# Add + gelu on one core: y in three loads instead of four, a new split of the adds, and a new order of VectorE's work around chunk 9

## Chip, cores, metric

The kernel runs on one core of a Trainium2 chip. The metric is the device time of one execution in microseconds (us). "Span" is the time inside one profiled execution; it is 1.5 to 1.9 us shorter than the metric for the same run.

Four words are used throughout. The profile counts 16 DMA engines for the core (its page gives the packets' time as a share of 16); a packet is one row of a DMA as one of them moves it. Each DMA here has 128 rows, and in the packet records they start in eight rounds of 16: eight for each DMA engine. A DMA lands when all of its data have arrived. Its lead is the time by which it is issued before the DMA ahead of it in the queue lands. A hand-over is the change from one DMA of the queue to the next.

## The reference

```python
batch, dim = 1024, 4096            # x and y are float32 [1024, 4096]
z = x + y
out = 0.5 * z * (1 + tanh(sqrt(2 / pi) * (z + 0.044715 * z**3)))    # float32
```

32 MiB are read (33.55 MB) and 16 MiB written (16.78 MB).

## The kernel before

Each of the 128 partitions holds 32768 columns of x. The sum and the result are made in place in `z`. The work goes in chunks of 2048 columns: an add (VectorE or GpSimd), `mag` = |z| and `gelu` = gelu(-|z|) on ScalarE into PSUM, and `end` = max(z, 0) + that, on VectorE. All DMAs are issued from one engine's queue, SyncE, in a fixed order.

```python
    YS = 8192                       # columns of one y buffer; two buffers
    CH = 2048
    PS = 2                          # PSUM buffers
    xloads = [16384, 16384]
    yloads = [8192, 8192, 8192, 8192]
    FIRST = 8
    stores = [16384, 10240, 6144]
    # chunk added by VectorE: the `end` in front of which it stands
    by_dve = {0: 0, 2: 0, 4: 2, 6: 4, 8: 8, 12: 10}
    # ... (cut)
    def store(i):
        a, b = sr[i]
        ins = nc.sync.dma_start(out=ov[:, a:b], in_=zt[:, a:b])
        if i == 0:
            tc.add_manual_dep(
                ins.ins, ends[FIRST].name, ...,
                reason="the stores join the queue when the last load is nearly done",
            )

    def add(c):
        eng = nc.vector if c in by_dve else nc.gpsimd
        eng.tensor_add(out=zt[:, a:b], in0=zt[:, a:b], in1=yt[s][:, o : o + b - a])
    # ... (cut)
    sp = [(load_y, 0), (load_x, 0), (load_y, 1), (load_x, 1), (load_y, 2), (load_y, 3)]
    sp += [(store, i) for i in range(len(stores))]
```

## Time and profile before

| | kernel before |
|---|---|
| time, median of 3 | 120.1 us (120.07 to 120.13) |
| span of the profiled run | 118.6 us |
| busy: VectorE, ScalarE, GpSimd | 50%, 51%, 47% |
| DMA queue busy | 98.6% |
| fourth y load lands | 79.85 us |
| stores issued at | 77.61, 96.34, 107.56 us |

Read it from the bottom. The last three rows say that the queue always has work and that every store is handed to it a few us (2.2 to 3.7) before it runs out. The engines' shares say little: they are averages over a first quarter with no compute at all and a rest with a good deal of it. The lines are in the prediction below.

### The profile page before, as it was taken

Reading aid. Unit: us, or ns where it says so; the run is one execution under the profiler, and the core shown is the slowest. Engines: PE = TensorE matmul, PEld = TensorE weight load, DVE = VectorE, ACT = ScalarE, POOL = GpSimd, SP = SyncE. Lnnn points to the kernel's source line nnn. Section 1 sums busy time; section 2 is a strip of 40 time slices with the busy share of each in tenths; the row PEclk is TensorE's granted clock in tenths of the full one; section 3 lists DMA queues with packets and bytes.
Section 4 is the critical chain, followed back from the end, with each engine's and each line's share of the span. In section 5 each row is a group of like instructions: output and inputs, shape, how many; then the busy total and the mean of one; then the engine's idle time right before and its main releaser. Section 6 shows DMA issues by size and latency. Waiting matters only on the chain.

```text
span 118.6 us, 160 instructions
## 1 busy us (share of the span) xinstructions
DVE 59.8 (50%) x24; ACT 60.8 (51%) x34; POOL 55.5 (47%) x14
## 2 busy tenths in 40 slices
DVE  0000000000399999699994594257999457742000
ACT  5000000000067979999379705797798999940000
POOL 0000000000399999997000029999999999100000
DMA  7989888998889988988899898998899889999996
GB/s 243 464 365 696 354 354 354 663 398 354 354 387 497 531 354 354 707 354 354 354 420 464 365 520 354 531 531 354 354 531 531 354 354 442 442 442 442 398 398 265
DMA packets 1296, 50.33 MB, mean 424 GB/s; under 512 B 144, under 2 KB 144, under 8 KB 144
## 3 DMA queue, kind: packets, MB, share of 16 engines
q1 hardware_dynamic: 1296, 50.33, 98.6%
HBM read 33.55 MB, written 16.78 MB: 424 GB/s over the span
## 4 chain that ended last, share of the span: by engine, by line
DMA 48%; POOL 34%; POOLq 4%; ACT 3%; DVE 2%; issue 0%; SPq 0%; DVEq 0%
POOL z L149 34%; DMA z<-in_x_dram 26%; DMA y<-in_y_dram 21%; POOLq L213 4%; DVE z L166 2%; ACT w L154 2%; ACT w L157 2%; SPq L132 0%; POOLq L149 0%; DVEq L166 0%
## 5 line engine op out<-in xcount | busy, mean ns | idle before, releaser
L149 POOL TENSOR_TENSOR z<-z,y 128x2048 f32<-128x2048 f32 x10 | 55.3, 5563 | 45.6 <-DMA z<-in_x_dram 31.1
L154 ACT ACTIVATE w<-z 128x2048 f32<-128x2048 f32 x16 | 30.1, 1880 | 42.5 <-DVE z L149 36.0
L166 DVE SCALAR_TENSOR_TENSOR z<-z,w 128x2048 f32<-128x2048 f32 (+1 forms) x17 | 36.4, 2157 | 16.0 <-ACT w L157 16.0
L149 DVE TENSOR_TENSOR z<-z,y 128x2048 f32<-128x2048 f32 x6 | 24.0, 4009 | 30.3 <-DMA z<-in_x_dram 30.1
L157 ACT ACTIVATE w<-w 128x2048 f32<-128x2048 f32 x16 | 29.8, 1862 | 0.5
L198 ACT ACT_TABLE_LOAD x1 | 1.3, 1283 | 1.3 <-PEq L230 1.3
L197 DVE MEMSET one<- 128x1 f32 x1 | 0.1, 59 | 1.3 <-PEq L230 1.3
L198 ACT ACTIVATE one<-one 128x1 f32<-128x1 f32 x1 | 0.2, 203 | 0.0
L230 POOL MEMSET const-float32-0.0<- 128x1 f32 x1 | 0.1, 98 | 0.2 <-issue 0.2
L230 POOL MEMSET const-bfloat16-1.0<- 128x1 bf16 x1 | 0.1, 101 | 0.0
L230 POOL MEMSET const-uint8-127<- 128x1 uint8 x1 | 0.1, 101 | 0.0
L230 POOL MEMSET const-float32-1.0<- 128x1 f32 x1 | 0.1, 98 | 0.0
## 6 DMA issues: line engine op xcount, KB each, us to landing
y<-in_y_dram SPq DMA_DIRECT2D x4, 4096.0 KB, 23.7
out_dram<-z SPq DMA_DIRECT2D x1, 5120.0 KB, 14.9
out_dram<-z SPq DMA_DIRECT2D x1, 3072.0 KB, 11.0
z<-in_x_dram SPq DMA_DIRECT2D x2, 44.9
out_dram<-z SPq DMA_DIRECT2D x1, 21.6
```

Source lines behind the costliest of these rows:

```text
L149: eng.tensor_add(out=zt[:, a:b], in0=zt[:, a:b], in1=yt[s][:, o : o + b - a])
L154: nc.scalar.activation(out=wt[c], in_=zt[:, a:b], func=act.Abs)
L157: nc.scalar.activation(out=wt[c], in_=wt[c], func=act.Gelu_apprx_tanh, scale=-1.0)
L166: ins = nc.vector.scalar_tensor_tensor(out=zt[:, a + o : a + o + n], in0=zt[:, a + o : a + o + n], scalar=0.0, in1=wt[c][:, o : o + n], op ...
L197: nc.vector.memset(one, 0.0)
L198: nc.scalar.activation(out=one, in_=one, func=act.Gelu_apprx_tanh)
L213: tc.compile()
L230: nc = _bacc.Bacc("TRN2", target_bir_lowering=False, num_devices=1)
```

## The change

The intent: one DMA fewer and a y buffer as large as fits, so that chunks 8 and 9 don't wait for a y load and only chunks 10 to 16 depend on the last one. Three of GpSimd's adds now wait for one of VectorE's (`turn`), so that the two engines run into each other less often: in the kernel before, while one of them added, an add of the other waited (VectorE's took 2.28 us alone and up to 6.59, GpSimd's 4.50 and up to 6.64; the prediction reads this from the trace). VectorE gets more of the last adds, and it ends chunk 9 before it adds chunks 10 and 11.

```diff
-    YS = 8192
+    YS = 20416
-    yloads = [8192, 8192, 8192, 8192]
-    FIRST = 8
+    yloads = [8192, 12224, 12352]        # the third over columns 0.. of the same buffer
+    FIRST = 9
-    ... [CH] * (TOT // CH)
+    ... [CH] * 9 + [CH - 64, 64] + [CH] * 6
-    by_dve = {0: 0, 2: 0, 4: 2, 6: 4, 8: 8, 12: 10}
+    by_dve = {0: 0, 2: 0, 4: 3, 6: 5, 10: 10, 11: 10, 12: 11, 14: 12, 16: 14}
+    turn = {1: 0, 13: 12, 15: 14}        # GpSimd's add waits for VectorE's
...
-                ends[FIRST].name,        # store 0 waits for half an `end` of chunk 8
+                gelus[FIRST].name,       # store 0 waits for half a `gelu` of chunk 9
...                                       # the halves move from `end` to `gelu`
```

Because of the chunk of 64 columns, later chunks have numbers one higher than before: 17 chunks, 0 to 16.

More of the change, by code (lines that the diff above doesn't have):

```diff
@@ L104, in ranges @@
         return [(e - f, e) for e, f in zip(ends, sizes)]
-    xr, yr, sr, cr = (ranges(r) for r in (xloads, yloads, stores, [CH] * (TOT // CH)))
+    xr, yr, sr, cr = (ranges(r) for r in (xloads, yloads, stores, [CH] * 9 + [CH - 64, 64] + [CH] * 6))
     C = len(cr)
-    by_dve = {0: 0, 2: 0, 4: 2, 6: 4, 8: 8, 12: 10}
+    by_dve = {0: 0, 2: 0, 4: 3, 6: 5, 10: 10, 11: 10, 12: 11, 14: 12, 16: 14}
+    turn = {1: 0, 13: 12, 15: 14}
     def over(rs, lo, hi):
@@ L114 @@
     pool_sb = ctx.enter_context(tc.tile_pool(name="xz", bufs=1))
-    pool_y = ctx.enter_context(tc.tile_pool(name="y", bufs=2))
     pool_w = ctx.enter_context(
@@ L120, with at_y @@
     zt = pool_sb.tile([P, TOT], fp32, tag="z", name="z")
-    yt, wt, ends = {}, {}, {}
+    yt = pool_sb.tile([P, YS], fp32, tag="y", name="y")
+    wt, adds, gelus = {}, {}, {}
+    def at_y(a):
+        return a - (yr[2][0] if a >= yr[2][0] else 0)
     def load_x(i):
@@ L128, in load_y @@
         a, b = yr[i]
-        s, o = divmod(a, YS)
-        if o == 0:
-            yt[s] = pool_y.tile([P, YS], fp32, tag="y", name=f"y{s}")
-        nc.sync.dma_start(out=yt[s][:, o : o + b - a], in_=yv[:, a:b])
+        o = at_y(a)
+        nc.sync.dma_start(out=yt[:, o : o + b - a], in_=yv[:, a:b])
     def store(i):
@@ L146, in add @@
         a, b = cr[c]
-        s, o = divmod(a, YS)
+        o = at_y(a)
         eng = nc.vector if c in by_dve else nc.gpsimd
-        eng.tensor_add(out=zt[:, a:b], in0=zt[:, a:b], in1=yt[s][:, o : o + b - a])
+        ins = eng.tensor_add(
+            out=zt[:, a:b], in0=zt[:, a:b], in1=yt[:, o : o + b - a]
+        )
+        adds[c] = ins.ins
+        if c in turn:
+            tc.add_manual_dep(
+                ins.ins,
+                adds[turn[c]].name,
+                mybir.DependencyInfo(mybir.DependencyClass.Sync, mybir.DependencyReason.DATA),
+                reason="the two engines take turns on their shared port",
+            )
     def mag(c):
         a, b = cr[c]
-        wt[c] = pool_w.tile([P, CH], fp32, tag="w", name=f"w{c}")
+        wt[c] = pool_w.tile([P, b - a], fp32, tag="w", name=f"w{c}")
         nc.scalar.activation(out=wt[c], in_=zt[:, a:b], func=act.Abs)
     def gelu(c):
-        nc.scalar.activation(
-            out=wt[c], in_=wt[c], func=act.Gelu_apprx_tanh, scale=-1.0
-        )
+        w_c = cr[c][1] - cr[c][0]
+        n = w_c // 2 if c == FIRST else w_c
+        for o in range(0, w_c, n):
+            w = wt[c][:, o : o + n]
+            ins = nc.scalar.activation(
+                out=w, in_=w, func=act.Gelu_apprx_tanh, scale=-1.0
+            )
+            gelus.setdefault(c, ins.ins)
     def end(c):
         a, b = cr[c]
-        parts = 2 if c == FIRST else 1
-        n = (b - a) // parts
-        for o in range(0, b - a, n):
-            ins = nc.vector.scalar_tensor_tensor(
-                out=zt[:, a + o : a + o + n], in0=zt[:, a + o : a + o + n], scalar=0.0,
-                in1=wt[c][:, o : o + n], op0=alu.max, op1=alu.add,
-            )
-            ends.setdefault(c, ins.ins)
-    sp = [(load_y, 0), (load_x, 0), (load_y, 1), (load_x, 1), (load_y, 2), (load_y, 3)]
+        nc.vector.scalar_tensor_tensor(
+            out=zt[:, a:b], in0=zt[:, a:b], scalar=0.0, in1=wt[c],
+            op0=alu.max, op1=alu.add,
+        )
+    sp = [(load_y, 0), (load_x, 0), (load_y, 1), (load_x, 1), (load_y, 2)]
     sp += [(store, i) for i in range(len(stores))]
@@ L183 @@
         load_y: lambda i: [
-            (add, c) for c in over(cr, yr[i][0] - 2 * YS, yr[i][1] - 2 * YS)
+            (add, c) for c in over(cr, 0, yr[2][1] - yr[2][0]) if i == 2
         ],
         add: lambda c: [(load_x, i) for i in over(xr, *cr[c])]
-        + [(load_y, i) for i in over(yr, *cr[c])],
+        + [(load_y, i) for i in over(yr, *cr[c])]
+        + ([(add, turn[c])] if c in turn else []),
         mag: lambda c: [(add, c)] + ([(end, c - PS)] if c >= PS else []),
@@ L190 @@
         end: lambda c: [(gelu, c)],
-        store: lambda i: [(end, c) for c in over(cr, *sr[i])] + [(end, FIRST)],
+        store: lambda i: [(end, c) for c in over(cr, *sr[i])] + [(gelu, FIRST)],
     }
```

## The prediction

Its sum: 116.3 + 2.3 = 118.6 us of span before, less 0.06 for the packets, so 118.5, and 120.05 of metric.

> **What bounds the kernel now.** I read the page's busy shares and its DMA queue first. Of each line below, "x" counts instructions, and the last figure of a DMA issue is the median time from issue to landing in us.
>
> ```profile
> span 118.6 us, 160 instructions
> ...
> DVE 59.8 (50%) x24; ACT 60.8 (51%) x34; POOL 55.5 (47%) x14
> ...
> DMA  7989888998889988988899898998899889999996
> ...
> q1 hardware_dynamic: 1296, 50.33, 98.6%
> ...
> y<-in_y_dram SPq DMA_DIRECT2D x4, 4096.0 KB, 23.7
> out_dram<-z SPq DMA_DIRECT2D x1, 5120.0 KB, 14.9
> out_dram<-z SPq DMA_DIRECT2D x1, 3072.0 KB, 11.0
> z<-in_x_dram SPq DMA_DIRECT2D x2, 44.9
> out_dram<-z SPq DMA_DIRECT2D x1, 21.6
> ```
>
> No compute engine works more than half the span; the one DMA queue is busy for 98.6% of it. So the suspect is the queue: 32 MiB read and 16 MiB written. Second, the chain of waits, for landings (start, duration):
>
> ```profile
> 0.43 30.92 DMA z<-in_x_dram
> ...
> 44.68 25.46 DMA y<-in_y_dram
> ```
>
> The first x load lands at 0.43 + 30.92 = 31.35, when 4.19 + 8.39 = 12.58 MB are in. The third y load lands at 70.14, at 29.36 MB. Between them 16.78 MB took 38.79 us: 432.6 GB/s. Third, the timeline for the stores' issues:
>
> ```profile
> 77.61 30.28 SPq L136 DMA_DIRECT2D out_dram<-z  x3
> ```
>
> The third store ends its issue at 77.61 + 30.28 = 107.89, so begins it (0.33 us) at 107.56 and lands 11.0 later, at 118.56. From 31.35 to there, 37.75 MB in 87.21 us: 432.9 GB/s, with no time lost at any hand-over. Hence the sum of the whole span: 50.33 MB / 432.8 GB/s = 116.3 us, and 2.3 us of start and last receipt, together 118.6. The chain blames POOL for 34% only because it goes through waits that end before the queue runs dry. Compute matters in one way: each DMA must be issued before its predecessor is through. The second y-buffer turn and the stores are the ones that wait for compute.
>
> How early is early enough? The fourth y load lands at 79.85 (issue 57.94 from the timeline, 21.9 in the DMA view of that window); store 0 is issued at 77.61, 2.24 before that, and lands at 77.61 + 21.6 = 99.2; 79.85 + 8.39 MB / 432.8 = 99.24. So a lead of 2.24 us over the predecessor's landing leaves no gap. Store 1, issued at 96.34, has 2.9 us; store 2 has 111.24 - 107.56 = 3.7 us.
>
> Fourth, the durations of adds, and how the two adders meet:
>
> ```profile
> L149 POOL TENSOR_TENSOR z<-z,y x10: 4502/5562/6635, 31.5 to 96.8; 128x2048 f32<-128x2048 f32 x10
> L149 DVE TENSOR_TENSOR z<-z,y x6: 2280/3636/6593, 31.5 to 83.0; 128x2048 f32<-128x2048 f32 x6
> ```
>
> ```profile
> 31.45 8.80 DVE L149 TENSOR_TENSOR z<-z,y 128x2048 f32<-128x2048 f32 x2 [30.06 <-DMA z<-in_x_dram]
> 31.49 13.16 POOL L149 TENSOR_TENSOR z<-z,y 128x2048 f32<-128x2048 f32 x2 [31.06 <-DMA z<-in_x_dram]
> 33.78 1.88 ACT L154 ACTIVATE w<-z 128x2048 f32<-128x2048 f32 x1 [31.02 <-DVE z L149]
> 35.69 1.86 ACT L157 ACTIVATE w<-w 128x2048 f32<-128x2048 f32 x1
> ...
> 40.18 2.27 DVE L166 SCALAR_TENSOR_TENSOR z<-z,w 128x2048 f32<-128x2048 f32 x1
> ```
>
> An add is 2.28 us on VectorE and 4.50 on GpSimd when alone. Two VectorE adds took 8.80 = 2.28 + 4.4 + 2.2: one ran, GpSimd ran, then the other.
>
> [...] the VectorE add, when waiting, was served before GpSimd's next one. The final op (one SBUF input, one PSUM) is 2.27-2.29 throughout and does not take part. [...] this trace has only 24, 32, 40 and 64 KB rows.
>
> **The change, part by part.**
> *Traffic.* The same bytes. y goes in three loads, not four: 128 packets (8 per DMA engine) and one completion fewer. The packet records show 1.212 us for 32 KB and 2.418 us for 64 KB, so about 6 ns a packet is fixed: 8 x 6 = 48 ns, and one 9 ns completion: 0.06 us saved, on the path.
> *Landings*, if the queue never idles, at 432.8 GB/s: x0 31.35; y1 (6.26 MB) 45.8; x1 65.2; y2 (6.32 MB) 79.8; store 0 99.2, store 1 111.3, store 2 118.5.
> *y2's issue.* It overwrites columns 0 to 12351 of y, so it waits for the adds of chunks 0 to 6 (64 columns of chunk 6). Adds 0, 1, 2, 3 run as before to 44.7. Add 5 (GpSimd) waits for y1 and runs 45.9 to 50.4. VectorE ends chunk 2 at 48.7 and its add 4 is held to 50.4, runs to 52.7; end 3 to 55.0. Chunk 4's two activations take 3.75: 56.5; its end 58.8; add 6 then runs to 61.1 [...]. y2 is issued at about 61.1: lead 4.1 us over x1's 65.2, against over 15 before (44.68 against 60.4), still above 2.24.
> *Store 0.* It now needs the first half of chunk 9's gelu. x1 65.2; add 8 to 69.8; add 9 (1984 columns) to 74.2; abs 1.83 to 76.0; half a gelu 0.95: issue at 77.0. Lead 2.8.
> *After y2.* End 9 runs to 80.2, so putting it ahead of adds 10 and 11 delays them by only 0.4 past the landing. Add 10 (64 columns) 0.1, add 11 to 82.6, end 10, add 12 to 84.9, add 13 (GpSimd, told to wait for add 12) to 89.4, add 14 to 91.7, add 15 (told to wait) to 96.2. ScalarE: chunk 11 from 82.65 to 86.4, chunk 12 to 90.1, chunk 13 to 93.9. End 13 to 96.2, store 1 issued at about 96.3: lead 2.9. Add 16 to 98.5, end 14 to 100.7, chunk 16's activations 101.4 to 105.15, end 107.45; store 2 issued at 107.5: lead 3.8.
> *Sum.* All four late issues keep a lead of at least 2.8 us, so nothing but the 0.06 us of packets reaches the end: 118.6 - 0.06 = 118.5 span. The metric was 120.1 for this span, so 120.05.
> The turns removed from contention and the extra ScalarE and VectorE pieces (one extra half gelu, a 64-column chunk: under 1 us together) lie beside the queue.
>
> **Rivals.**
> *A bubble at y2.* [...] everything behind moves 4.5 us: y2 at 65.6, a bubble of 65.6 + 2.2 - 65.2 = 2.6 at most, time up to 122.6. Against it: each of the three VectorE adds in the trace that had to wait was served next.
> *A bubble at the stores.* Chunks 11 to 16 now all start after 79.8, where before four chunks could start at 70.2. If the ScalarE sequence slips by 1 us, store 1's lead falls to 1.9 and a gap of at most 0.3 us appears: 120.4. For it: store 1 needs three whole chunks in the 16.5 us after y2's landing; against: the sum above, with the durations of before, ends at the same 107.5 as before.
> *Odd row sizes cost DMA rate.* y1 and y2 are 12.6 MB, 29 us; a loss of 2% there would be 0.6 us: 120.6. Nothing in the trace speaks for it; the five sizes of packets that it has all fit one line.
> *Faster by an early start of compute.* Chunks 8 and 9 no longer wait for a y load. But compute isn't what ends last, so it gives nothing; 120.0.
>
> **Range and chances.** The bytes set a floor near 120.0, and the runs of before spread by 0.06, so below 119.8 is hard to reach. Above, a small bubble or row loss gives 120.4 to 120.6. Range 119.8 to 120.6. Faster by 2% would need 117.7, 2.4 us under the floor: 0.01. Slower by 2% needs 122.5, only the y2 rival: 0.03. Within 2%: 0.96.
>
> **What would show it.** The share of the DMA queue stays at 98 to 99%; y2's issue near 61, store issues near 77, 96.3 and 107.5; landing of store 0 near 99.2; VectorE's add 4 ending near 52.7. Wrong would be: a landing of store 0 later than y2's landing plus 19.4 us, a y2 issue after 63, or y1 landing later than 45.9.

## The result

| | before | changed |
|---|---|---|
| time, median of 6 | 120.11 us (120.02 to 120.72) | 120.16 us (120.08 to 120.64) |
| ratio | | 1.0002, 95% interval 0.9977 to 1.0027 |
| span of the profiled run | 118.6 us | 118.7 us |

The time is the same.

The page of the changed kernel, the lines that answer to those of before:

```profile
span 118.7 us, 160 instructions
...
DVE 55.2 (47%) x27; ACT 61.1 (51%) x37; POOL 40.1 (34%) x12
...
DMA  7989888988899798988896899698899889999996
...
q1 hardware_dynamic: 1152, 50.33, 98.6%
...
y<-in_y_dram SPq DMA_DIRECT2D x1, 6176.0 KB, 19.0
y<-in_y_dram SPq DMA_DIRECT2D x1, 6112.0 KB, 44.6
out_dram<-z SPq DMA_DIRECT2D x1, 5120.0 KB, 15.1
...
out_dram<-z SPq DMA_DIRECT2D x1, 3072.0 KB, 11.2
...
out_dram<-z SPq DMA_DIRECT2D x1, 22.3
```

128 packets are gone (1296 to 1152 counts also the 16 completions of one DMA), the bytes are not, and the queue is as busy as it was. GpSimd lost 15 us of busy time and the end did not notice. The timeline of SyncE's queue has the issues (start, duration, and how many were merged into the line):

```profile
61.01 0.33 SPq L137 DMA_DIRECT2D y<-in_y_dram  x1
77.04 30.77 SPq L141 DMA_DIRECT2D out_dram<-z  x3
```

and the same view cut to the time around store 1:

```profile
96.28 0.34 SPq L141 DMA_DIRECT2D out_dram<-z  x1
```

y2 is issued at 61.01, store 0 at 77.04, store 1 at 96.28 and store 2 at 77.04 + 30.77 - 0.33 = 107.48. The prediction had 61.1, 77.0, 96.3 and 107.5. y2 lands at 61.01 + 19.0 = 80.0, store 0 at 77.04 + 22.3 = 99.3, the last store at 107.48 + 11.2 = 118.7. Where GpSimd's 15 us went is in the view of the adds:

```profile
L154 DVE TENSOR_TENSOR z<-z,y x9: 217/2285/3030, 31.5 to 96.2; 128x2048 f32<-128x2048 f32 x8, 128x64 f32<-128x64 f32 x1
L154 POOL TENSOR_TENSOR z<-z,y x8: 4367/4518/6577, 33.9 to 91.8; 128x2048 f32<-128x2048 f32 x7, 128x1984 f32<-128x1984 f32 x1
```

The median add is now the lone one on both engines (2.285 and 4.518 us, against 3.636 and 5.562 before). From these durations I estimate that about 9 of the 15 us are work that went to VectorE (two adds fewer on GpSimd) and about 6 are waiting for VectorE's adds that was inside the durations of GpSimd's and is now gone or an explicit wait. Some 4 us of it are left on GpSimd: its longest add still takes 6.577 us.

### The profile page after: what moved, and what is told of

The parts are those of the page before. It is cut to its first block, busy times and chain, and to the rows that moved or that the text cites. A ratio compares the mean times of both kernels' runs of the same rounds, so it can differ in the third digit from the quotient of the medians.

```text
span 118.7 us, 160 instructions
## 1 busy us (share of the span) xinstructions
DVE 55.2 (47%) x27; ACT 61.1 (51%) x37; POOL 40.1 (34%) x12
## 2 busy tenths in 40 slices
DMA packets 1152, 50.33 MB, mean 424 GB/s; under 512 B 128, under 2 KB 128, under 8 KB 128
## 3 DMA queue, kind: packets, MB, share of 16 engines
q1 hardware_dynamic: 1152, 50.33, 98.6%
## 4 chain that ended last, share of the span: by engine, by line
DMA 38%; POOL 17%; ACT 15%; DVE 10%; another core or an unknown queue 7%; issue 3%; DVEq 0%
DMA y<-in_y_dram 38%; POOL z L154 17%; ACT w L169 8%; ACT w L176 7%; DVE z L183 6%; DVE z L154 5%; DVEq L183 0%
## 5 line engine op out<-in xcount | busy, mean ns | idle before, releaser
L154 POOL TENSOR_TENSOR z<-z,y 128x2048 f32<-128x2048 f32 (+1 forms) x8 | 39.9, 5002 | 56.0 <-DVE z L154 46.6
L169 ACT ACTIVATE w<-z 128x2048 f32<-128x2048 f32 (+2 forms) x17 | 30.2, 1779 | 42.2 <-DVE z L154 37.3
L183 DVE SCALAR_TENSOR_TENSOR z<-z,w 128x2048 f32<-128x2048 f32 (+2 forms) x17 | 36.7, 2159 | 20.7 <-ACT w L176 20.7
L154 DVE TENSOR_TENSOR z<-z,y 128x2048 f32<-128x2048 f32 (+1 forms) x9 | 19.4, 2171 | 30.1 <-DMA z<-in_x_dram 30.1
L176 ACT ACTIVATE w<-w 128x2048 f32<-128x2048 f32 (+2 forms) x18 | 30.1, 1672 | 0.6
## 6 DMA issues: line engine op xcount, KB each, us to landing
y<-in_y_dram SPq DMA_DIRECT2D x1, 4096.0 KB, 12.1
out_dram<-z SPq DMA_DIRECT2D x1, 3072.0 KB, 11.2
out_dram<-z SPq DMA_DIRECT2D x1, 22.3
```

Source lines behind the costliest of these rows:

```text
L154: ins = eng.tensor_add(out=zt[:, a:b], in0=zt[:, a:b], in1=yt[:, o : o + b - a])
L169: nc.scalar.activation(out=wt[c], in_=zt[:, a:b], func=act.Abs)
L176: ins = nc.scalar.activation(out=w, in_=w, func=act.Gelu_apprx_tanh, scale=-1.0)
L183: nc.vector.scalar_tensor_tensor(out=zt[:, a:b], in0=zt[:, a:b], scalar=0.0, in1=wt[c], op0=alu.max, op1=alu.add,)
```

## The experiments

The theory to test: the DMA queue's bytes set the time, and compute counts only through the moment at which each DMA is issued. The rivals: compute is on the path after all; a gain and a loss cancel; the number or the size of the loads matters by itself. Each experiment is an edit of the changed kernel unless it says otherwise. "Base" is the kernel before, run in the same rounds.

### 1. The queue alone

```diff
-    queues = [sp, pool, acts, dve]
+    queues = [sp]          # no adds, activations, ends: wrong on purpose
# y2 waits for the two earlier y loads, each store for its x load
```

> All adds, activations and ends removed (the result is wrong on purpose): the same eight transfers, each issued as early as its data allow. Theory (the DMA queue's bytes and its fixed 2.3 us are the whole time, compute is hidden): 120.0 to 120.2, the same as before and after. Rival (the chain of adds and activations, which the profile's chain names, takes part in the end): clearly less, 118 or under.

Measured: 121.14 us (120.89 to 121.16), base 120.08, ratio 1.0081, interval 1.0066 to 1.0096. The result is wrong, as intended.

Neither came in. Compute is not on the path: without it the time does not fall. But it rose by 1.0 us, which the theory had no room for and which has to be explained before the run counts as proof. The timeline of the queue, then two lines of the page's issues:

```profile
45.89 0.33 SPq L137 DMA_DIRECT2D y<-in_y_dram  x1
46.27 19.75 SPq L141 DMA_DIRECT2D out_dram<-z  x3
```

```profile
y<-in_y_dram SPq DMA_DIRECT2D x1, 6176.0 KB, 34.8
...
out_dram<-z SPq DMA_DIRECT2D x1, 3072.0 KB, 53.8
```

y2 lands at 45.89 + 34.8 = 80.7, not at 80.0. All three stores were queued by 66.02 (46.27 + 19.75), with no wait left, and yet the last lands at 119.4. The packet records of the trace place the loss: y2 has eight 49408 B packets on each DMA engine; a normal one takes 1.82 us; those that started between 74 and 78 us, the last two of each engine, took up to 2.85, together 0.90 us too long per engine. From there on everything is late by about that. In the changed kernel the same packets lose less than 0.01 us. So I formed a second theory: a store that already stands in the queue slows the last packets of the load ahead of it. Runs 7, 9, 10 and 11 test it.

### 2. The named order undone: adds 10 and 11 ahead of the end of chunk 9

```diff
-    by_dve = {..., 10: 10, 11: 10, ...}
+    by_dve = {..., 10: 9, 11: 9, ...}
```

> Only the order on VectorE changed: adds of chunks 10 and 11 ahead of the end of chunk 9. Theory (leads of the stores decide): end 9 moves from 80.4 to 84.8, chunk 11's abs from 82.7 to 84.9, store 1's issue from 96.3 to 98.7, its lead over store 0's landing from 3.0 to 0.6 us; a gap of about 0.9 us opens in front of store 1; 121.0. Rival (compute has slack for it or the issue needs no lead): 120.1.

Measured: 120.37 us (120.32 to 120.6), base 120.08, ratio 1.0024, interval 1.001 to 1.0037.

```profile
80.10 2.43 DVE L154 TENSOR_TENSOR z<-z,y 128x64 f32<-128x64 f32 x2 [4.19 <-DMA y<-in_y_dram]
...
82.45 2.35 DVE L183 SCALAR_TENSOR_TENSOR z<-z,w 128x1984 f32<-128x1984 f32 x2
84.69 1.88 ACT L169 ACTIVATE w<-z 128x2048 f32<-128x2048 f32 x1 [3.87 <-DVE z L183]
...
98.25 0.34 SPq L141 DMA_DIRECT2D out_dram<-z  x1
```

This timeline shows the chain as expected: the ends of chunks 9 and 10 come after the adds, ScalarE's next abs waits for them and starts at 84.69, and store 1 is issued at 98.25 instead of 96.28. The direction was right, the size a third of the 0.9 us: the issue was 0.45 us earlier than I had put it, and its first packet started at 99.09, 0.84 us after the issue. So the order that the change names is worth 0.3 us.

### 3. y2 issued one chunk later

```diff
-    by_dve = {..., 6: 5, ...}
+    by_dve = {..., 6: 6, ...}
```

> Only add 6 moved behind end 5 on VectorE, so that the third y load is issued at about 64.7 and not 61.0, against x1's landing at 65.2. Theory: the load's first packet comes about 1 us after its issue, x1's last packet ends at 64.7, so a gap of 1.1 us that nothing regains: 121.2. Rival (an issue before the predecessor's landing leaves no gap): 120.1.

Measured: 122.35 us (122.25 to 122.82), base 120.08, ratio 1.019, interval 1.0171 to 1.021.

```profile
64.71 0.33 SPq L137 DMA_DIRECT2D y<-in_y_dram  x1
78.58 31.61 SPq L141 DMA_DIRECT2D out_dram<-z  x3
```

The issue is where it was expected, and the gap too: y2's first packet starts at 65.66, 0.95 us after the issue, and a DMA engine stood still for 1.3 us on average (x1's last packets end at 64.59 on average, y2's first start at 65.91). But the loss is 2.3 us, twice the expectation. The packet records give the rest: on 14 of the 16 DMA engines the first y2 packet took 2.44 to 2.82 us where 1.82 is the rule, while the other two began it only at 66.85 and 67.17 and took 1.82; that is 0.68 a DMA engine on average. The last packets lost 0.24, with store 0 queued about 3.5 us ahead of the landing that they would have had (the last one began at 79.93; with the usual 1.82 and 0.34 to the landing it would have been 82.1). That is 2.2 us on average over the 16 DMA engines. In this run the load that started after a pause cost more than the pause. The first packets of the whole kernel, the first y load's after nothing, are slow as well: 1.92 us on average in the changed kernel where 1.21 is usual.

### 4. No turns between GpSimd and VectorE

```diff
-    turn = {1: 0, 13: 12, 15: 14}
+    turn = {}
```

> The three waits that make GpSimd's adds 1, 13 and 15 follow VectorE's adds are gone. Theory: GpSimd takes add 13 at 80.1, ahead of VectorE's adds 10 and 11, which are then held by 4.4 us (VectorE served next twice) or 8.9 us (GpSimd's add 15 in between); ScalarE's chunk 11 and store 1 move by as much; store 1's gap is 2.9 or 7.4 us: 123 or 127.5. Rival ([...] the queue is the bound): 120.1.

Measured: 126.95 us (126.0 to 127.2), base 120.08, ratio 1.0555, interval 1.0522 to 1.0587.

```profile
79.88 8.95 POOL L154 TENSOR_TENSOR z<-z,y 128x2048 f32<-128x2048 f32 x2 [5.76 <-DMA y<-in_y_dram]
80.25 10.73 DVE L154 TENSOR_TENSOR z<-z,y 128x64 f32<-128x64 f32 x2
...
91.01 1.88 ACT L169 ACTIVATE w<-z 128x2048 f32<-128x2048 f32 x1 [6.05 <-DVE z L154]
```

In this timeline GpSimd runs adds 13 and 15 back to back from y2's landing; VectorE's adds 10 and 11, worth 2.4 us alone, take 10.73, and ScalarE's chunk 11 starts at 91.01 instead of 82.72. The second of my two cases came in: GpSimd's waiting add 15 ran between VectorE's two (ScalarE's chunk 10, which waits for the first of them, starts at 84.49). Store 1 is issued at 104.57 and the queue stands still for 6.9 us. The waits that look like lost time on GpSimd hold up the whole split of the work.

### 5. The three loads alone, with the adds split as before

```diff
-    by_dve = {0: 0, 2: 0, 4: 3, 6: 5, 10: 10, 11: 10, 12: 11, 14: 12, 16: 14}
-    turn = {1: 0, 13: 12, 15: 14}
+    by_dve = {0: 0, 2: 0, 4: 2, 6: 4, 8: 8, 13: 11}
+    turn = {}
```

> The three y loads and the 64-column chunk of the change, but VectorE's and GpSimd's shares of the adds as in the kernel before, and no turns. Theory: after y2's landing at 79.9 GpSimd has five whole adds of 4.5 us and VectorE one: add 13 at 87, add 12 at 91.7, store 1 issued near 101.5, a gap of about 3.2 us in front of it and perhaps 0.4 in front of store 0: 123.7. Rival (three loads instead of four are free by themselves): 120.1.

Measured: 123.73 us (123.64 to 123.77), base 120.07, ratio 1.0299, interval 1.028 to 1.0317.

```profile
79.94 24.72 POOL L154 TENSOR_TENSOR z<-z,y 128x64 f32<-128x64 f32 x6 [10.22 <-DMA y<-in_y_dram]
...
101.08 0.34 SPq L141 DMA_DIRECT2D out_dram<-z  x1
```

As expected to 0.03 us. With the big last load six of seventeen chunks start only at 80 us, and GpSimd's row of adds lasts to 104.7. Store 1 is issued at 101.08, its first packet starts at 101.92 (0.84 later) and the queue was idle for 3.2 us. So the change is two parts that cancel: the larger last load costs 3.7 us with the old split, and the new split, turns and order win it back. What they win back is not a gain over the kernel before, which never had that problem: there the last load held back four chunks, not six and a sliver, since the third y load had landed at 70.1.

### 6. The last store late on purpose, by one and by three adds

```diff
+        if c == C - 1:
+            for _ in range(N):     # N = 1 or 3; store 2 waits for the last
+                ins = nc.vector.tensor_add(
+                    out=yt[:, 0:CH], in0=yt[:, 0:CH], in1=yt[:, 0:CH])
```

> One extra add of 2.28 us on VectorE after the last end, on which the last store waits: issue at 109.8, not 107.5; lead over store 1's landing 1.6 us in place of 3.9. Theory (the first packet needs about 1 us after the issue, store 1's last packet ends at 110.7 to 111.1): no gap or 0.1 us, 120.1 to 120.2. Rival (the chain of compute sets the end): 2.3 us more, 122.4.

Measured: 120.23 us (119.98 to 120.29), base 120.07, ratio 1.0007, interval 0.9993 to 1.002.

> Three such adds: issue at 114.4. Theory: first packet at 115.4 against store 1's last at 110.8: a gap of 4.5 us, 124.6. Rival (chain of compute): 6.8 us more, 126.9. The measured loss gives the latency from issue to first packet.

Measured: 124.83 us (124.83 to 124.94), base 120.07, ratio 1.0396, interval 1.0377 to 1.0414.

The timeline of the first, then of the second:

```profile
107.45 2.29 DVE L197 TENSOR_TENSOR y<-y 128x2048 f32<-128x2048 f32 x1
109.77 0.33 SPq L142 DMA_DIRECT2D out_dram<-z  x1
```

```profile
107.40 6.94 DVE L197 TENSOR_TENSOR y<-y 128x2048 f32<-128x2048 f32 x3
114.36 0.33 SPq L142 DMA_DIRECT2D out_dram<-z  x1
```

2.3 us more on the very last compute step cost nothing that the runs can resolve, 6.9 us more cost 4.8: the difference is the slack that the queue had. This settles the rival of the compute chain. In the second run the first packet of the store starts at 115.20, 0.84 us after the issue, and the first two packets of each DMA engine take 0.92 and 0.94 us where 0.91 is usual: this store, started after a pause, cost little but the pause, unlike the load of run 3.

### 7. Store 0 not held back

```diff
-        if i == 0:
-            tc.add_manual_dep(ins.ins, gelus[FIRST].name, ...)
+        # no such wait: store 0 goes when end 7 is done
```

> Store 0 no longer waits for chunk 9's half gelu: issued when end 7 is done, at about 70.9 and not 77.0, while y2 still has 9 us to run. Theory (one queue, served in order): 120.1, y2 lands at 79.9 as now. Rival (the kernel's own comment: the store then mixes with the load): y2 lands later, up to 9 us, compute moves with it and store 1 is late: 121 to 127.

Measured: 121.09 us (120.92 to 121.15), base 120.07, ratio 1.0077, interval 1.0063 to 1.0092. The timeline of the queue, and y2's line in the page's issues:

```profile
60.90 0.33 SPq L137 DMA_DIRECT2D y<-in_y_dram  x1
70.73 37.73 SPq L141 DMA_DIRECT2D out_dram<-z  x3
```

```profile
y<-in_y_dram SPq DMA_DIRECT2D x1, 6176.0 KB, 20.0
```

The rival came in, at its lower end: y2 lands at 80.9, 0.9 us later, with the loss (1.0 us a DMA engine) again in the last two packets of each DMA engine. It is not a mixing over the whole 9 us in which the store waits: the packets that start between 70.7 and 74 are as fast as ever; y2's last packets but one begin in the same column, at 75.2 us, in both views below. The DMA view from 74 to 81 us shows it, in the changed kernel and then here. A column is 0.175 us, and in a view this short a group of digits marks where packets begin:

```profile
DMA  6600000999960000009996000000999980000000
```

```profile
DMA  0000000899900000000999978000000000999900
```

The last three groups are y2's last two packets and the first of store 0. In the changed kernel they begin 11 and 10 columns apart, here 12 and 15, and in the packet records each first packet of the store begins where a last packet of y2 has ended.

### 8. y in four again

```diff
-    yloads = [8192, 12224, 12352]
+    yloads = [8192, 12224, 6208, 6144]
```

> The changed kernel with its third y load cut into two of 24 KB rows: one DMA and 128 packets more than it, as many as before. Theory (the number of loads is worth 0.06 us): 120.1 to 120.3. Rival (three loads bring a gain that something else takes back): 120.5 or more.

Measured: 120.22 us (120.06 to 120.54), base 120.09, ratio 1.0003, interval 0.9984 to 1.0021. The number of loads makes no difference that these runs can resolve. The 0.06 us that I had worked out is a quarter of the interval's half width and is neither shown nor refuted.

### 9. Store 0 a little later

```diff
-            gelus.setdefault(c, ins.ins)     # the first half
+            gelus[c] = ins.ins               # the second half
```

> Store 0 waits for the second half of chunk 9's gelu: issue at 78.0, not 77.0, 1.9 us ahead of y2's landing. Two earlier runs (queue_alone, stores_free) issued it at 46 and 71 and lost 1.0 us each, all of it in the last two y2 packets of each DMA engine (up to 2.85 us where 1.82 is the rule). Theory (a store that is queued while the last load still runs slows that load's last packets, the less the later it comes; the first packet needs 0.9 to 1.0 us after the issue): no slow packet at all, no gap, 119.9 to 120.1. Rival (the loss is of another kind): as the changed kernel, 120.1 to 120.2, or later.

Measured: 120.13 us (119.96 to 120.83), base 120.09, ratio 1.0005, interval 0.9982 to 1.0027. Store 0 was issued at 77.98, y2 landed at 79.9, no packet near the end was slow, no gap appeared. It is as fast as both kernels; the interval is too wide to call it better.

### 10. Store 0 a little earlier

```diff
-                gelus[FIRST].name,
+                ends[8].name,
```

> Store 0 waits for the end of chunk 8: issue at 76.0, 3.9 us ahead of y2's landing. Theory: part of the slow packets, between the 0.0 to 0.1 us of issue 77.0 and the 1.0 us of issue 70.7: 120.3 to 120.9, with y2 landing at 80.1 to 80.7. Rival (only an issue many packets ahead does harm): 120.1.

Measured: 120.81 us (120.51 to 120.91), base 120.09, ratio 1.0049, interval 1.0032 to 1.0065. The timeline of the queue, and y2's line in the issues:

```profile
60.88 0.33 SPq L137 DMA_DIRECT2D y<-in_y_dram  x1
75.88 32.41 SPq L141 DMA_DIRECT2D out_dram<-z  x3
```

```profile
y<-in_y_dram SPq DMA_DIRECT2D x1, 6176.0 KB, 19.8
```

Within the expected range, near its upper end. An issue at 75.88 loses 0.7 us; with one at 77.04, in the changed kernel, the last two packets of a DMA engine lose less than 0.01. The edge lies in between, near the time at which the load's last packets begin (77.19 to 77.83 in the changed kernel). Two runs above lie in between as well: 0.05 us was lost in run 2 (issue at 76.96, lead 2.9 to 3.0), and 0.24 in run 3 (lead about 3.5).

### 11. The kernel before, its store 0 not held back

The same edit as in run 7, on the kernel before.

> The kernel before, with its store 0 no longer held for chunk 8's end: issue at 70.0 and not 77.6, 9.9 us ahead of the fourth y load's landing. Theory (any load whose successor in the queue is a store loses at its end): the last 32 KB packets take longer than 1.21 us, landing up to 80.9, 120.6 to 121.2. Rival (only the new 48 KB rows suffer): 120.1, no 32 KB packet over 1.3 us there.

Measured: 121.19 us (121.01 to 121.35), base 120.09, ratio 1.0082, interval 1.0067 to 1.0098. The timeline of the queue:

```profile
70.09 37.93 SPq L136 DMA_DIRECT2D out_dram<-z  x3
```

Its last y load has 32 KB rows; those packets that started at 76 to 80 us took up to 2.3 us instead of 1.21 and it landed at 80.96. So it is not the new row sizes: the last load pays here too when store 0 is queued long behind it.

### One that could not be built

y in 8192 + 12288 + 12288 columns, without the chunk of 64, was refused while building:

```
Not enough space for pool "xz" with 208.03125 kb per partition ... There was 207.8740234375 kb per partition left
```

By that message, 207.874 KiB less the 128 of z leave 79.87 for y, of which 20416 columns take 79.75. It settles why there is a chunk of 64 columns, which the prediction could only guess (the guess is cut there); it is no statement on its time.

## Why the prediction was right

**The bound.** The prediction's sum (50.33 MB at 432.8 GB/s and 2.3 us) holds: the changed kernel's queue has no gap, and runs 1 and 6 show that neither taking compute away nor adding 2.3 us to its end moves the time down or up through compute itself. No loss from the new row sizes; the changed kernel's packet records now show it: 1.806 us (median) for the 48896 B rows and 1.825 for those of 49408 B, on the line through 0.912 for 24 KB and 1.514 for 40 KB.

**Landings and issues.** All four issues came within 0.1 us of the working, and the landings within 0.2. So the chains of adds, activations and ends, worked out from durations of the kernel before, can be trusted to that size as long as the order on each engine and the turns between the two adders are kept.

**One detail of the working was wrong without harm.** "Adds 0, 1, 2, 3 run as before to 44.7": VectorE now ran adds 0 and 2 back to back, and GpSimd's add 1, told to wait for add 0, waited for add 2 as well (it took 6.49 us from 33.90; add 2 ended at 36.02). Add 3 still ended at 44.84: the four adds together took as long as before (13.3 us, 13.2 before).

**The turns of the adds.** The rival of a bubble at y2 rested on GpSimd's add 7 going before add 4. It did not: add 4 took 2.50 us at 50.11. But run 4 shows that "VectorE is served next" is no safety between two VectorE adds (10.73 us for 2.4 us of work). (The sum under the adds' lines, 2.28 + 4.4 + 2.2, makes 8.88 and not 8.80; nothing hangs on it.)

**The 0.06 us of packets** could not be seen. In the profiled run one DMA engine landed y2 0.2 us behind the rest, which is more. The packet records put that at y2's first packets (up to 2.08 us instead of 1.82), not at store 0; in run 4, where y2 was issued at the same time, they show none of it. So I take it for chance, which is not shown.

**What the prediction had too simple** is its rule that a lead of 2.24 us or more over the predecessor's landing "leaves no gap", as if more lead were always safe. It held for these four issues. The lower edge was nearer than 2.24: a store issued 1.7 us ahead was free (run 6), and first packets started 0.84 to 0.95 us after their issue. Between a load and a store the lead has an upper edge as well. Counted to the landing that an undisturbed load has, 79.9 us (82.1 in run 3), a lead of 1.9 to 2.9 us was free, 3.5 cost 0.2 us, 4.0 cost 0.7, 9.2 and more cost 0.9 to 1.0. The working did not know this edge, so that the 2.9 of store 0 fell just short of it was luck. Between loads, or between stores, there is none in these runs: x1 was queued 44 us ahead of y1's landing, and in run 1 stores 1 and 2 were queued 35 and 46 us ahead, and took 12.1 and 7.3 us, the plain 5.24 and 3.15 MB at 433 GB/s. The rival "a bubble at y2" was undersized too, as run 3 shows: by its rule an issue at 64.71 costs 64.7 + 2.2 - 65.2 = 1.7 us, and 2.3 were measured. It counted the pause (too long, at 2.2 us from issue to start) and not the slow packets behind it.

**Why it isn't faster.** The change shortens what was hidden: GpSimd's busy time fell from 55.5 to 40.1 us, and one DMA went. No version tried beats both kernels. With the queue busy from its first packet at 1.0 us to the end of its last at 118.3 (118.1 before) there is no gap left to close, and the inputs and the output are fixed. Of the 2.3 us that the prediction adds to the bytes, the changed kernel's records show 1.0 before the first packet, 0.7 in the slow first packet of each DMA engine and 0.4 after the last packet; no run tried to shorten these.

**What stays open** is why a store behind a load slows the load's end. The runs show where (the last two packets of each DMA engine), how much, and when it is avoided; they do not show the mechanism. In every such run the store was the same store 0 of 64 KB rows, so whether its size matters is not tested.

## What to carry to other kernels

When one DMA queue is busy from start to end, test the bound by taking compute away and by making the last step late on purpose, before working on the engines' shares. Then look at each hand-over: here a DMA had to be issued about 1 us (0.84 to 0.95) before its predecessor's last packets ended, and a store that follows a load not more than about 3 us before that load's landing. Judge a larger load by what it does to the work that must follow it: here it cost 3.7 us that a new split of the adds had to win back.
